# Two transformer blocks on one core: the order of sixteen experts' products, and the rows in which their weights arrive

## The chip, the cores and the metric

The kernel runs on one core of a Trainium2 chip. The metric is the device time of one execution in microseconds (us), as the median of several runs. A profile is one further execution that the hardware profiler took; its engines are PE (TensorE's matmuls), PEld (TensorE's weight loads), DVE (VectorE), ACT (ScalarE), POOL (GpSimd) and SP (SyncE, which here issues transfers only).

## The reference

A sequence of 512 tokens of width 1024 goes through two blocks in float32. The first block (a gated linear recurrence, an mLSTM, a cross attention, an MLP) and the attention half of the second are not touched by the change. What is touched is the second block's expert layer and what follows it:

```python
def expert_choice_ffn(xn, w_router, w_gate, w_up, w_down):   # 16 experts, cap = 64 tokens each
    aff = jax.nn.softmax(jnp.einsum('bsd,de->bse', xn, w_router).astype(jnp.float32), axis=-1)
    top_aff, top_idx = lax.top_k(jnp.swapaxes(aff, 1, 2), cap)
    xg = xn[bidx, top_idx]
    hid = jax.nn.silu(jnp.einsum('becd,edf->becf', xg, w_gate)) * jnp.einsum('becd,edf->becf', xg, w_up)
    y = jnp.einsum('becf,efd->becd', hid, w_down) * top_aff[..., None].astype(xn.dtype)
    return jnp.zeros((B, S, D), dtype=y.dtype).at[bidx, top_idx].add(y)
# then: h = h + sigmoid(rmsnorm(h) @ w_ple_gate) * (p @ w_ple), and a last rmsnorm
```

Each expert has three matrices of 1024 x 1024 in float32, 4 MB each; the sixteen together are 201 MB, and each is read once.

## The kernel before

The residual `x` lies in SBUF as four tiles of 128 tokens. The experts go in pairs, since two times 64 chosen tokens fill 128 partitions. For a pair, `gather` builds a one-hot matrix `oh` on DVE (L1351), and `rows(k)` multiplies it with the tokens on PE, 128 columns of the model at a time (L1360: four matmuls, each of which the profile shows as two); ACT copies each result into `xg` (L1361). `affinities` (L1366) picks the 128 affinities with the same one-hot, and four transposes turn the one-hot into `gT` (L1457).

For each expert, the gate and the up product (L1445) take eight steps `k` each, with 64 tokens as stationary operand and two halves of 512 columns; a step is four matmul records. DVE and ACT make `hd = silu(gate) * up` (L1460 to L1462), PE transposes it (L1465), ACT copies that into `hT` (L1467), and the down product (L1471) takes eight steps more. Its result, times the affinity, is kept in two parts, `yh` (ACT, L1479) and `yl` (DVE, L1480). After the second expert of a pair, `scatter` sends `yh` and `yl` back through `gT` (L1483, L1484), and DVE adds the eight results into `x` (L253). After expert 15 the adding is merged with the first half of the next projection (L1492 to L1510); before that, PE turns `x` into `xT` (L1530). Beside expert 5 the small product `p @ w_ple` is made (`project_p`, L1386).

PSUM has eight banks: four of tag `d` (`pd`: gate, up, scatter), two of tag `s` (`pscore`: down, gather rows, affinities) and two of tag `o` (`pout`: transposes).

Weights arrive in pieces of 1 MB, two steps `k` each, issued on SP's queue (L804, L806). Fifteen buffers in a ring (`wnext` 12, `wlast` 3) take them; six places that are still free at the start (`spare`: `act_hi`, `pp`, four `y4` tiles) take the first extra ones, so that 21 MB can lie ready. In HBM each matrix has rows of 4 KB, so a piece is 256 packets of 4 KB.

The program's text gives priorities. A planner of the framework sets the order of each engine's instructions ahead of the run, from its own estimate of when operands are ready; semaphores then hold each instruction until they are. On the chip each engine follows that order. The order written before is, for each expert: gather (even experts), gate and up, hidden, transposes, down, scatter (odd experts); gather rows are written between the steps of the gate product, and the last pair's gather stands after expert 11's gate and up (L1448).

Of the kernel before, what the change touches and what calls it, by code (L numbers as in the profile page):

```python
# [19 lines left out]
P = 128  # L20
# [15 lines left out]
def two_blocks_kernel(ctx: ExitStack, tc: tile.TileContext, A: dict, out: bass.AP, stage: int = 99):  # L36
# [751 lines left out]
    turn = itertools.cycle(["wnext"] * 12 + ["wlast"] * 3)  # L788
# [7 lines left out]
    def load_pieces(e, got):  # L796

        for n in ("w_exp_gate_2", "w_exp_up_2", "w_exp_down_2"):
            wv = A[n][0, e].rearrange("(k p) f -> p k f", p=P)
            for k in range(0, KT, 2):  # L800
                w = spare.pop(0) if e < 2 and len(got) >= 16 + 4 * e else w8()
                if isinstance(w, list):
                    for i in range(2):
                        nc.sync.dma_start(w[i], wv[:, k + i, :])  # L804
                else:
                    nc.sync.dma_start(w, wv[:, k:k + 2, :])  # L806
                    w = [w[:, 0, :], w[:, 1, :]]
                got += w
                yield

    spare = []
    started = {}

    def start_expert(e, n):

        if e not in started:
            got = []
            started[e] = got, load_pieces(e, got)  # L820
        for _ in itertools.islice(started[e][1], n):
            pass

    def load_expert(e):
        start_expert(e, 12)
        return started[e][0]


    with ExitStack() as blk:
# [440 lines left out]
        open_ring(late, "wnext", 12, side="right")  # L1270
        start_expert(0, 6)

        def more():
            start_expert(0, 8 - 6)
            start_expert(1, 4)
# [32 lines left out]
    with ExitStack() as blk:  # L1308
        pool = blk.enter_context(tc.tile_pool(name="moe", bufs=1, reuse_waits="tile"))
        open_ring(blk, "wlast", 3)  # L1310

        def y4(dt=F32, shape=(D,)):
            return pool.tile([P] + list(shape), dt, name="y4", tag="y4", bufs=5)

        def m2(dt=F32, shape=(T,)):
            return pool.tile([P] + list(shape), dt, name="m2", tag="m2", bufs=4)
# [5 lines left out]
        def pick(ahead=False):  # L1322
            if ahead:
                return m2(shape=(NT, 2, CAP)), y4(shape=(2, KT, CAP))
            return (pool.tile([P, NT, 2, CAP], F32, name="oh", bufs=1),
                    pool.tile([P, 2, KT, CAP], F32, name="xg", bufs=1))

        picked = [pick()]
        w = acts_half(F32, (NT, D), "act_hi")
        spare += [w[:, 0:2, :], w[:, 2:4, :], [y4(), y4()], [y4(), y4()]]  # L1330
# [5 lines left out]
        spare += [w[:, 0:2, :], w[:, 2:4, :]]  # L1336
        ws = load_expert(0)
# [3 lines left out]
        def gather(g):  # L1341

            oh, xg = picked.pop() if picked else pick(ahead=2 * g + 2 == NE)
# [11 lines left out]
            src, sel = (xn[0], oh) if g else (x, scaled)  # L1355

            def rows(k):
# [13 lines left out]
            return oh, xg, rows, affinities  # L1371

        def load_p():
# [4 lines left out]
            return pr, raw  # L1378

        def split8(raw):  # L1380
            hi, lo = w8(dt=F32R), w8(dt=F32R)
            S.copy(hi, raw)
            V.tensor_sub(lo, raw, hi.bitcast(F32))
            return hi, lo

        def project_p(pr, raw):  # L1386
            wh, wl = split8(raw)
            pT = w8((2, 2, T), F32R)
# [41 lines left out]
        oh = xg = None  # L1430
        for e in range(NE):
            if e == NE - 1:
                gfin = row(y4(), A["norm_final_2"])
# [225 lines left out]
```

## Time and profile before

| | us |
|---|---|
| runs: median (lowest, highest) | 1955.38 (1954.65, 1956.43) |
| profiled execution | 1954.67 |
| its span in the profile | 1952.9 |
| PE busy | 1878.2 |
| DVE busy | 919.1 |
| ACT busy | 718.4 |

The span is the time from the first to the last instruction that the profile shows. Busy times overlap between engines. A busy PE is not PE at its peak: matmuls are pipelined and a record holds its drain, so starts must be compared, not lengths. "Idle before" names what released an instruction. The experts begin at 1383.5 us with the first gather, and the last down product ends at 1890 us; 63 us follow.

### The profile page before, as it was taken

What the parts mean: (1) busy time and instruction counts of PE and PEld (TensorE: products, weight loads), DVE (VectorE), ACT (ScalarE), POOL (GpSimd) and SP (SyncE); (2) the same over time, 40 slices, a digit from 0 to 9 for tenths busy, and PEclk for the clock granted to TensorE, in tenths of its full rate; (3) what the DMA queues carried; (4) which work ended last, traced back from release to release, by engine and by line L of the source; (5) the groups of instructions that cost most, each with busy time, mean ns of one, the idle gap of its engine ahead of it and who ended that gap; (6) DMA issues with size and microseconds to landing.
All of it is one profiled execution on the core that took longest, in us unless ns stands there. A gap on an engine that the chain in (4) does not pass through costs nothing. (4 is left out here: it accounts for less than half of the span.)

```text
span 1952.9 us, 24468 instructions
## 1 busy us (share of the span) xinstructions
PE 1878.2 (96%) x9723; PEld 1362.9 (70%) x9723; DVE 919.1 (47%) x1659; ACT 718.4 (37%) x1329; POOL 66.9 (3%) x103
## 2 busy tenths in 40 slices
PE   7999999999999999999999999999699999999998
PEld 6777788888888888887787778887344354444346
DVE  5777777465543443436875564453322111111236
ACT  4454774343332322325665554322121121111134
POOL 0000220000000000002000000000000000000000
PEclk9999999999999999999999999999799999999999
DMA  7222226431233333324222222236889999998951
GB/s 206 55 64 72 56 85 189 131 107 55 73 111 98 97 97 97 97 76 112 73 65 57 74 71 70 86 125 247 325 312 402 375 381 401 406 405 334 409 237 44
DMA packets 178052, 330.88 MB, mean 169 GB/s; under 512 B 10766, under 2 KB 90370, under 8 KB 177938
## 3 DMA queue, kind: packets, MB, share of 16 engines
q1 hardware_dynamic: 177522, 328.91, 48.1%
q8 instruction: 77, 1.26, 0.3%
q0 software_dynamic: 416, 0.41, 0.1%
q14 instruction: 37, 0.30, 0.0%
HBM read 327.19 MB, written 2.10 MB: 169 GB/s over the span
## 5 line engine op out<-in xcount | busy, mean ns | idle before, releaser
L104 DVE TENSOR_TENSOR lo<-raw,hi 128x1024 fp32r<-128x1024 f32 x208 | 253.5, 1221 | 324.5 <-ACT hi L103 321.5
L103 ACT CAST hi<-raw 128x1024 fp32r<-128x1024 f32 x208 | 218.0, 1049 | 417.7 <-PE pd L126 230.7
L124 PE MATMUL pd<-hi,act_hi 128*128 128x512 f32 (+2 forms) x584 | 228.2, 391 | 2.0 <-ACT act_hi L206 1.6
L125 PE MATMUL pd<-lo,act_hi 128*128 128x512 f32 (+2 forms) x584 | 226.5, 388 | 0.8 <-DVE lo L104 0.8
L124 PE MATMUL pd<-act_hi,hi 128*128 128x512 f32 (+1 forms) x592 | 224.2, 380 | 0.5 <-ACT act_hi L206 0.5
L126 PE MATMUL pd<-act_hi,lo 128*128 128x512 f32 (+1 forms) x592 | 224.5, 380 | 0.0
L125 PE MATMUL pd<-act_lo,hi 128*128 128x512 f32 (+1 forms) x592 | 224.3, 379 | 0.0
L1445 PE MATMUL pd<-w,xg 128*64 128x512 f32 x896 | 205.3, 598 | 0.0
L126 PE MATMUL pd<-hi,act_lo 128*128 128x512 f32 (+1 forms) x512 | 199.8, 392 | 0.0
L1445 PEld LDWEIGHTS pd<-w,xg 128*64 128x64 f32 x896 | 60.8, 137 | 109.0 <-issue 100.3
L124 PEld LDWEIGHTS pd<-hi,act_hi 128*128 128x128 f32 x584 | 110.3, 189 | 22.7 <-ACT act_hi L206 3.3
L126 PEld LDWEIGHTS pd<-act_hi,lo 128*128 128x128 f32 x592 | 111.5, 188 | 19.5 <-issue 0.2
L125 PEld LDWEIGHTS pd<-act_lo,hi 128*128 128x128 f32 x592 | 111.5, 188 | 19.4 <-DVE act_lo L207 0.5
L124 PEld LDWEIGHTS pd<-act_hi,hi 128*128 128x128 f32 x592 | 111.1, 188 | 19.9 <-ACT act_hi L206 1.0
L125 PEld LDWEIGHTS pd<-lo,act_hi 128*128 128x128 f32 x584 | 110.2, 189 | 20.1 <-DVE lo L104 1.3
L1471 PE MATMUL pscore<-w,m 128*64 128x512 f32 x464 | 107.9, 607 | 6.7 <-ACT m L1467 6.7
L126 PEld LDWEIGHTS pd<-hi,act_lo 128*128 128x128 f32 x512 | 96.7, 189 | 17.9 <-DVE act_lo L207 0.4
L1480 DVE SCALAR_TENSOR_TENSOR y<-pscore,affs,y 64x512 fp32r<-64x512 f32 x32 | 24.0, 750 | 169.2 <-ACT y L1479 168.9
L253 DVE TENSOR_TENSOR x<-x,pd 128x512 f32<-128x512 f32 x111 | 71.9, 684 | 61.9 <-PE pd L126 56.7
L125 PE MATMUL pd<-lo,hh 128*128 128x512 f32 x256 | 99.7, 390 | 0.0
L124 PE MATMUL pd<-hi,hh 128*128 128x512 f32 x256 | 99.7, 389 | 0.0
L126 PE MATMUL pd<-hi,hl 128*128 128x512 f32 x256 | 99.6, 389 | 0.0
(459 smaller groups left out, 2870.9 us busy)
## 6 DMA issues: line engine op xcount, KB each, us to landing
w<-in_w_exp_gate_dram SPq DMA_DIRECT2D x64, 1024.0 KB, 9.1
w<-in_w_exp_up_dram SPq DMA_DIRECT2D x64, 1024.0 KB, 13.8
w<-in_w_exp_down_dram SPq DMA_DIRECT2D x58, 1024.0 KB, 9.0
raw<-in_w_in_dram SPq DMA_DIRECT2D x80, 512.0 KB, 3.6
raw<-in_w_up_dram SPq DMA_DIRECT2D x32, 512.0 KB, 4.2
raw<-in_w_down_dram SPq DMA_DIRECT2D x32, 512.0 KB, 3.6
raw<-in_w_xkv_dram SPq DMA_DIRECT2D x16, 512.0 KB, 4.9
raw<-in_w_out_dram SPq DMA_DIRECT2D x16, 512.0 KB, 3.7
```

Source lines behind the costliest of these rows:

```text
L103: S.copy(hi[:, :size], raw[:, :size])
L104: V.tensor_sub(lo[:, :size], raw[:, :size], hi[:, :size].bitcast(F32))
L124: PE.matmul(ps, ah, bh, start=first, stop=False)
L125: PE.matmul(ps, ah, bl, start=False, stop=False)
L126: PE.matmul(ps, al, bh, start=False, stop=last)
L253: return lambda t, ps: V.tensor_add(x[:, t, c:c + 512], x[:, t, c:c + 512], ps)
L1445: PE.matmul(ps[64 * half:64 * half + 64, :], xg[:, e % 2, k, :], ws[i + k][:, 512 * half:512 * half + 512], start=(k == 0), stop=(k == KT ...
L1471: PE.matmul(py[64 * half:64 * half + 64, :], hT[:, k % 4, 64 * (k // 4):64 * (k // 4) + 64], ws[16 + k][:, 512 * half:512 * half + 512], s ...
L1480: V.scalar_tensor_tensor(yl[r0:r0 + 64, 512 * half:512 * half + 512], src, sc, h.bitcast(F32), op0=OP.mult, op1=OP.subtract)
```

## The change

The experts are pipelined by one: `hidden(e)` (gate and up of expert e) stands ahead of `down(e-1)`, and `turned(e)` (the transposes and their copy) behind it. Scatters of the pair before are called between every second step of an odd expert's gate and up product. Rows of the next gather are called between the steps of the down product of the pair's first expert (for the last pair, the turns of `x`). Gather rows go to `pout`, four in one bank, and no longer to `pscore`; the turned one-hot goes to `pscore`. Loads come in the order of use, gate and up of e+1 ahead of down of e, and a counter (`room`) issues each when its buffer's user is written. The host stacks the three matrices into one tensor in which a piece is contiguous, 8 KB for each partition. `y4` has 4 buffers for 5, `m2` 3 for 4, and `gT` a tile of its own. The three work buffers of the `p` product are now taken when its loads are issued.

```diff
+    order = [(0, m) for m in range(2)]
+    for e in range(1, NE):
+        order += [(e, 0), (e, 1), (e - 1, 2)]
+    order.append((NE - 1, 2))
+    order = [(e, m, q) for e, m in order for q in range(KT // 2)]
+    pieces = {(e, m): [] for e in range(NE) for m in range(3)}
+    homes = {}
+    loads = iter(enumerate(order))
+    room = [WNEXT + WLAST]
+
+    def load(n):
+        for i, (e, m, q) in itertools.islice(loads, n):
+            wv = A["w_exp"][e, m, q]
+            if i in homes:
+                w = homes[i]
+            else:
+                w = w8()
+                room[0] -= 1
...
+                nc.sync.dma_start(w.rearrange("p a b -> p (a b)"), wv.rearrange("p a b -> p (a b)"))
...
+    def used(e, m):
+        room[0] += sum(r for _, r in pieces.pop((e, m))) // 2
+        load(max(0, room[0]))
...
             def rows(k):
-                ps = pscore()[:, :P]
+                j = k % 4
+                if j == 0:
+                    ps[0] = pout()
                 for t in range(NT):
-                    PE.matmul(ps, src[:, t, k * P:(k + 1) * P], sel[:, t, :], start=(t == 0), stop=(t == NT - 1))
-                S.activation(xg[:, :, k, :], ps.rearrange("p (e s) -> p e s", e=2), AF.Copy, scale=gcol[:, k:k + 1])
+                    PE.matmul(ps[0][:, j * P:(j + 1) * P], src[:, t, k * P:(k + 1) * P], sel[:, t, :],
+                              start=(t == 0), stop=(t == NT - 1))
+                S.activation(xg[:, :, k, :], ps[0][:, j * P:(j + 1) * P].rearrange("p (e s) -> p e s", e=2), AF.Copy,
+                             scale=gcol[:, k:k + 1])
...
+            def back():
+                gT = pool.tile([P, T], F32R, name="gT", bufs=1)
+                pt = pscore()
+                for t in range(NT):
+                    PE.transpose(pt[:, t * P:(t + 1) * P], oh[:, t, :], ident)
+                S.copy(gT, pt)
+                return gT
...
+        def hidden(e, xg, between):
             pg, pu = pd(), pd()
-            for i, ps in ((0, pg), (8, pu)):
+            for m, ps in enumerate((pg, pu)):
                 for k in range(KT):
...
+                    for f in between.get(KT * m + k, ()):
+                        f()
+            for m in range(2):
+                used(e, m)
             hd = m2()
             S.activation(hd, pg, AF.Sigmoid)
             V.tensor_mul(hd, hd, pg)
             V.tensor_mul(hd, hd, pu)
+            return hd
+        def turned(e, hd):
             pt = pout()
             for i in range(4):
                 PE.transpose(pt[:, i * P:(i + 1) * P], hd[:, i * P:(i + 1) * P], ident)
-            hT = m2(shape=(4, P))
-            S.copy(hT, pt.rearrange("p (a b) -> p a b", a=4))
+            hT[e] = m2(shape=(4, P))
+            S.copy(hT[e], pt.rearrange("p (a b) -> p a b", a=4))
+        def down(e, yh, yl, between):
+            h = hT.pop(e)
             py = pscore()
             for k in range(KT):
...
+                for f in between.get(k, ()):
+                    f()
+            used(e, 2)
...
+        hd = hidden(0, xg, each([lambda k=k: rows(k) for k in range(1, KT)], range(KT - 1)))
+        turned(0, hd)
+        for e in range(1, NE):
             if e == 5:
+                room[0] -= 5
+            todo = [lambda t=t, n=n: scatter(t, n, pd()) for n in range(2) for t in range(NT)] if e % 2 and e > 1 else []
+            hd = hidden(e, xg, each(todo, range(0, 16, 2)))
...
+            more = {}
+            if e % 2:
+                affinities()
+                gT = back()
+                yh, yl = y4(F32R), y4(F32R)
+                if e + 1 < NE:
+                    xg, rows, affinities, back = gather((e + 1) // 2)
+                    more = each([lambda k=k, f=rows: f(k) for k in range(KT)], range(KT))
+                else:
+                    wgr = [load_gate(k) for k in range(0, KT, 2)]
+                    xT = [w8((4, T)) for _ in range(2)]
+                    more = each([lambda t=t, i=i: turn_x(t, i) for t in range(NT) for i in range(2)], range(KT))
+            if e == 6:
+                pp = project_p(*praw)
+                room[0] += 5
+            down(e - 1, yh, yl, more)
+            if e == 5:
+                praw = load_p()
+            turned(e, hd)
+        gfin = row(y4(), A["norm_final_2"])
+        down(NE - 1, yh, yl, {})
...
+    w = np.stack([given.pop(f"w_exp_{n}_2")[0] for n in ("gate", "up", "down")], 1)
+    given["w_exp"] = w.reshape(NE, 3, KT // 2, 2, P, D).transpose(0, 1, 2, 4, 3, 5)
```

## Rows read from the trace of the kernel before

**Rows 1.** The page: busy tenths of PE and DMA in 40 slices.
```profile
PE   7999999999999999999999999999699999999998
...
DMA  7222226431233333324222222236889999998951
```

**Rows 2.** Window: length, busy us of PE, PEld, DVE, ACT, POOL; clock, DMA, GB/s.
```profile
1387.00:1890.00 503.00, 480.06 (x2394) 216.78 (x2392) 89.35 (x151) 88.71 (x191) 0.00 (x0) 0.99 0.95 374
```

**Rows 3.** L1445's waits (us, times), then waits of SP (total, times, longest).
```profile
  DMA w<-in_w_exp_gate_dram: 2.3, 8
...
SPq L806 <- PE pd L1445: 258.3, 111, 19.7
```

**Rows 4.** Waits of PE, 1387 to 1890: total us, times, longest.
```profile
PE pout L1465 <- DVE m L1462: 11.5, 12, 2.8
PE pscore L1471 <- ACT m L1467: 6.7, 14, 0.9
PE pscore L1360 <- ACT xg L1361: 1.6, 4, 0.5
PE pscore L1360 <- ACT y L1361: 1.1, 1, 1.1
```

**Rows 5.** PE's timeline, experts 8 and 9: start, length, line, operation, idle before.
```profile
1661.70 5.37 PE L1445 MATMUL pd<-w,xg 128*64 128x512 f32 x24
1667.87 0.66 PE L1465 MATMUL pout<-ident,m 128*128 128x128 f32 x4 [0.79 <-DVE m L1462]
1669.25 7.09 PE L1471 MATMUL pscore<-w,m 128*64 128x512 f32 x32 [0.73 <-ACT m L1467]
1676.17 13.90 PE L1445 MATMUL pd<-w,xg 128*64 128x512 f32 x64
...
1692.19 1.94 PE L1471 MATMUL pscore<-w,m 128*64 128x512 f32 x8 [0.24 <-ACT m L1467]
1694.06 1.16 PE L1360 MATMUL pscore<-oh,act_hi 128*128 128x128 f32 x8
1695.15 1.94 PE L1471 MATMUL pscore<-w,m 128*64 128x512 f32 x8
...
1703.87 0.94 PE L1360 MATMUL pscore<-oh,act_hi 128*128 128x128 f32 x6
```

**Rows 6.** PE's timeline, end of expert 6.
```profile
1600.98 0.64 PE L1457 MATMUL pout<-ident,oh 128*128 128x128 f32 x4
...
1614.97 13.90 PE L1445 MATMUL pd<-w,xg 128*64 128x512 f32 x64
```

**Rows 7.** PE's timeline: affinities of expert 2, scatters after experts 7 and 13.
```profile
1460.13 8.80 PE L1445 MATMUL pd<-w,xg 128*64 128x512 f32 x40
...
1469.86 1.07 PE L1445 MATMUL pd<-w,xg 128*64 128x512 f32 x2
...
1643.53 1.20 PE L1483 MATMUL pd<-y,m 128*128 128x512 f32 x4
...
1645.48 0.38 PE L1360 MATMUL pscore<-oh,act_hi 128*128 128x128 f32 x2
...
1649.49 4.51 PE L1445 MATMUL pd<-w,xg 128*64 128x512 f32 x20
...
1834.41 1.21 PE L1483 MATMUL pd<-y,m 128*128 128x512 f32 x4 [0.78 <-ACT y L1479]
...
1839.99 1.51 PE L1445 MATMUL pd<-w,y 128*64 128x512 f32 x6
```

**Rows 8.** PE's timeline, end of expert 15.
```profile
1877.61 1.09 PE L1530 MATMUL pout<-ident,x 128*128 128x128 f32 x8
...
1882.93 7.09 PE L1471 MATMUL pscore<-w,m 128*64 128x512 f32 x32 [0.68 <-ACT m L1467]
```

**Rows 9.** DMA: a burst of 2 KB rows, a stretch of 4 KB rows.
```profile
DMA packets 285, 0.55 MB, mean 367 GB/s; under 512 B 16, under 2 KB 16, under 8 KB 285
...
DMA packets 2120, 8.20 MB, mean 410 GB/s; under 512 B 120, under 2 KB 120, under 8 KB 2119
```

More of the change, by code (lines that the diff above doesn't have):

```diff
@@ L1370, in affinities @@
                         S.copy(affs[64 * half:64 * half + 64, e:e + 1], ps[64 * j:64 * j + 64, e:e + 1])
-            return oh, xg, rows, affinities
+            def back():
[5 more added lines that the diff above has]
+                return gT
+            return xg, rows, affinities, back
         def load_p():
@@ L1481, in two_blocks_kernel @@
                                        op0=OP.mult, op1=OP.subtract)
-            def scatter(t, n, ps):
-                PE.matmul(ps, gT[:, t * P:(t + 1) * P], yh[:, 512 * n:512 * n + 512], start=True, stop=False)
-                PE.matmul(ps, gT[:, t * P:(t + 1) * P], yl[:, 512 * n:512 * n + 512], start=False, stop=True)
-                add_to_x(512 * n)(t, ps)
-            last = e == NE - 1 and stage > 7
-            if e % 2 and not last:
-                for n in range(2):
-                    for t in range(NT):
-                        scatter(t, n, pd())
@@ L1511, in two_blocks_kernel, with scatter, each @@
-            if e == 4:
-                praw = load_p()
+        def scatter(t, n, ps):
+            PE.matmul(ps, gT[:, t * P:(t + 1) * P], yh[:, 512 * n:512 * n + 512], start=True, stop=False)
+            PE.matmul(ps, gT[:, t * P:(t + 1) * P], yl[:, 512 * n:512 * n + 512], start=False, stop=True)
+            add_to_x(512 * n)(t, ps)
+        def each(fs, places):
+            b = {}
+            for f, i in zip(fs, places):
+                b.setdefault(i, []).append(f)
+            return b
@@ L1513, in two_blocks_kernel, with turn_x @@
+        def turn_x(t, i):
+            ps = pout().rearrange("p (a b) -> p a b", a=4)
+            for k in range(4):
+                PE.transpose(ps[:, k, :], x[:, t, (4 * i + k) * P:(4 * i + k + 1) * P], ident)
+            S.copy(xT[i][:, :, t * P:(t + 1) * P], ps)
+        xg, rows, affinities, back = gather(0)
+        rows(0)
+        hd = hidden(0, xg, each([lambda k=k: rows(k) for k in range(1, KT)], range(KT - 1)))
+        turned(0, hd)
+        for e in range(1, NE):
             if e == 5:
-                pp = project_p(*praw)
@@ new lines, in two_blocks_kernel @@
+            if e == 6:
[7 more added lines that the diff above has]
+        down(NE - 1, yh, yl, {})
+        zh, zl = [[w8((4, T), F32R) for _ in range(2)] for _ in range(2)]
+        wg = []
+        pss = [pd() for _ in range(NT)]
+        todo = [(t, n) for n in range(2) for t in range(NT)]
+        for k in range(KT):
+            ps = pout()
+            PE.matmul(ps, yh[:, k * P:(k + 1) * P], gT, start=True, stop=False)
+            PE.matmul(ps, yl[:, k * P:(k + 1) * P], gT, start=False, stop=True)
+            zk, hi = xT[k // 4][:, k % 4, :], zh[k // 4][:, k % 4, :]
+            V.tensor_add(zk, zk, ps)
+            S.copy(hi, zk)
+            V.tensor_sub(zl[k // 4][:, k % 4, :], zk, hi.bitcast(F32))
+            if k % 2:
+                wg.append(split_gate(k // 2, wgr[k // 2]))
+                gate_step(pss, k // 2)
+                for _ in range(2):
+                    scatter(*todo.pop(0), pscore())
```

139 lines of the change are left out of this document (34 added, 105 removed).

## The prediction

> **What bounds the kernel now.** I read the page's slices first, then the windows, then the waits, then PE's timeline. The slices say that PE and the DMA engines are both full in the last third of the span [rows 1], so one must find which of them waits for the other. The window over the experts, 1387 to 1890 us, has PE busy 480.06 of 503 us at 374 GB/s [rows 2]. The waits decide. PE's gate and up products stood for a landing 8 times, 2.3 us in all, while the loads stood 258.3 us, 111 times, for those same products to free a buffer [rows 3]. Weights lie ready and transfers wait for PE: the stage is paced by TensorE and by what stops it. Two waits stop it: the transposes of the hidden tile wait 11.5 us for VectorE's product, and the down product 6.7 us for ScalarE's copy of the transposes [rows 4]. That is one chain per expert: gate and up, VectorE, four transposes, copy, down.
>
> How much time lies behind the chain? 374 GB/s over 503 us are 188.1 MB; in a full stretch the queue moves 410 GB/s [rows 9], so these bytes need 459 us and could end at 1846. PE can save 44 us before transfers set the end, even if rows move no faster than now.
>
> **The change, part by part.** Sums are for the profiled execution, 1954.67 us with a span of 1952.9; the median of the runs is 1955.38, so 0.7 is added at the end. Steps between starts: an expert matmul 0.213 us (13.90 for 64 less 5.37 for 24, over 40), a gather matmul or a transpose 0.11 (1.16 for 8 less 0.94 for 6, over 2) [rows 5], a scatter matmul 0.244 (1643.53 to 1645.48 for 8) [rows 7].
>
> *The hidden chain goes.* In the new order gate and up of expert e+1 run before the down product of e, and the transposes of e+1 after it, so the chain lies beside a product of some 7 us. Its price today, from start to start: expert 8 goes from 1661.70 to 1669.25, 7.55 us for 24 matmuls and four transposes worth 5.55: 2.00 lost. Expert 9 goes from 1676.17 to 1692.19, 16.02 for 64 matmuls and eight transposes worth 14.51: 1.51 [rows 5]. There are 5 like the first (experts 4, 8, 10, 12, 14) and 7 like the second (1 to 13, odd). Expert 6 is worse: 1600.98 to 1614.97 is 13.99 for eight transposes and 32 matmuls worth 7.70, 6.29 lost [rows 6]; the longest single wait, 2.8, is there [rows 4]. Expert 15: 1877.61 to 1882.93 is 5.32 for 28 transposes worth 3.08, 2.24 lost [rows 8]. Experts 0 and 2 have other work there already. Sum 10.0 + 10.6 + 6.3 + 2.2 = 29.1. The four transposes still interrupt products, and such a visit costs 0.33 (affinities inside the gate product: 1460.13 to 1469.86 is 9.73 for 40 and 8 matmuls worth 9.40 [rows 7]), so 14 x 0.33 = 4.6 stays. Gain 24.5.
>
> *The scatter moves into the next gate and up product.* Expert 13's scatter waited for its results and VectorE's adds: 1834.41 to 1839.99 is 5.58 for 16 matmuls worth 3.90 [rows 7]. Gain 1.7. The other six lose little today, as gather matmuls fill them: 1643.53 to 1649.49 is 5.96 for 16 scatter and 16 gather matmuls worth 5.66 [rows 7], 0.30 each, 1.8 in all. Woven in, 56 scatters of two matmuls each interrupt a product. As single visits at the gather's 0.38 (below) that is 21.3 - 1.8 = +19.5; with two to a visit (two of four pd banks are free beside gate and up) 28 x 0.33 - 1.8 = +7.4; if they fell only where PE stands, -1.8. I take +7.4, nearest to today's rows, which have scatters in clusters.
>
> *The gather moves into the down product.* It is interleaved already: 8 down matmuls and a row of 8 gather matmuls take 2.96 (1692.19 to 1695.15), worth 2.58, so 0.38 a visit [rows 5]. I count 49 visits to products in the timeline; the new program writes 63 (7 in the first gate product, 56 in down products): +5.3 as written, 0 if the planner joins rows as it does today, -12 if it joined most. I take half, +2.6. The waits of today's rows for ScalarE, 1.6 + 1.1 [rows 4], go, as 0.85 of product stands between two rows: gain 2.7.
>
> *Small ones.* The 8 turns of x become visits: 8 x 0.33 = +2.6. The last expert's transposes stand right ahead of its down product with nothing beside them: 1.38 (1667.87 to 1669.25) less 0.44 of transposes [rows 5], +0.9. The down product needs one of two score banks, and the affinities and the turned one-hot take both just ahead of it: 0 to 0.4 eight times, I take 1.0. One y4 and one m2 buffer fewer: in the tail at most three gated tiles live, and y4 holds the last pair, the final gain and junk; 0, at worst one 0.7 us VectorE step. The five p buffers leave ten pieces of the ring, as now, loads come in the order of use, and SP only loads here: 0, covered by weights that lie ready.
>
> *8 KB packets.* No weight row of 8 KB is in the trace. Full stretches give 367 GB/s at 2 KB and 410 at 4 KB [rows 9]: 89 and 160 ns a packet, which goes on to about 301 ns at 8 KB, an estimate of 436 GB/s. From below stands the 2 KB row, 367. I take the nearest, 410, and 0 us: PE waits for no weights, and the 44 us are cover. Without it the stage would take 188.1 MB at the rate that comes.
>
> Sum: removed 24.5 + 1.7 + 2.7 = 28.9; added 7.4 + 2.6 + 2.6 + 0.9 + 1.0 = 14.5. Net -14.4: 1940.3, and 1941 against the median. With the high ends (19.5, 5.3, 2.6, 0.9, 3.2) it is +2.6; with the low ends (-1.8, 0, 2.6, 0.9, 0) -27.2, and -39 if the gather's visits are joined as well.
>
> A page bears on the visits. A visit costs 0.33 and 0.38 us in the trace [rows 5, 7]. The Trainium skill, "TensorE: Matmul & The Clock Gate", Part 2, has PE's queue draw the next weight load ahead of running matmuls, so that it overlaps. By that rule visits would be free, as in the fast rival; the trace disagrees on the price.
>
> **The rivals.**
> 1. *Gather rows queue on one bank (slower).* Four rows now share one pout bank, and each is copied out alone. Before, a row with no product ahead of it waited up to 0.5 for ScalarE's copy [rows 4]. 48 rows follow another in the same bank; all of them back to back cost 48 x 0.5 = 24: 1965. It decides from 29 of the 48. For it: the planner puts ready work where it expects PE to stand. Against: the program has a product step between two rows. The Trainium skill, "PSUM — Partial Sum Buffer", "PSUM bank collisions raise a hardware error", wants PE's writes and another engine's reads kept apart by bank, not by address. By that rule disjoint columns would wait too; no row here shows two engines in one bank. Chance 0.12.
> 2. *Work is regrouped (faster).* The planner sets PE's order; today gather rows stand among scatters that were written earlier [rows 7]. With more ready work it may join rows and scatters: the low ends, 27 to 39 less, 1917 to 1929. Against it: a single xg, and two free pd banks. Chance 0.17.
> 3. *The chain stays in part.* If the planner sets the transposes right behind their own product, half of the 24.5 remains: -2.2, 1953. For it: they become ready early. Against: the down product is written first and its weights are there. Chance 0.15.
> 4. *Transfers set the pace (slower).* If 8 KB rows moved at the 2 KB row's 367, 188.1 MB would take 512.5 us, 9.5 more than the stage now: 1965. It decides below 385 GB/s (188.1 MB in 488.6 us). Against it: the rate rises with the size. Chance 0.06.
>
> **The numbers.** Forecast 0.50, 1941, its own range 1932 to 1950. About 0.2% (3.9 us) is what a measurement tells from no change. Faster (under 1951.5): forecast 0.49, rival 2 0.17, rival 3 0.07, rival 1 in part 0.01, 0.74. Within: 0.01, rival 3 0.07, rivals 1 and 4 0.02 each, 0.12. Slower: rival 1 0.09, rival 4 0.04, rival 3 0.01, 0.14. The range 1924 to 1959 leaves out the fast end of rival 2 and the full price of rivals 1 and 4, some 0.2 together.
>
> **What would show it.** Right: PE's waits for VectorE and ScalarE ahead of transposes and down products, 18.2 us now, fall under 4; the stage's 503 us become some 489; the loads still wait for PE; the 63 us after the last down product stay. Rival 1 shows as gather matmuls that wait for xg's copies, rival 3 as the old two waits at half their sum, rival 4 as weight loads that wait for landings. The forecast is wrong if a visit to a product costs much other than 0.33 to 0.38, or if PE's order is not the program's.

## The result, and the profile after

The changed kernel takes 1970.21 us (median of four runs, 1969.27 to 1972.07) against 1955.02 for the kernel before on the same chip: a ratio of 1.0080, 95% interval [1.0068, 1.0093]. It is slower by some 15 us, where 14 less were forecast. Times of experiments are given as ratios to the kernel before, run on the same chip, which took 1953.5 to 1955.9 us there; differences in us are differences of these ratios times 1955. The interval of one ratio is some 0.0013 to either side, so the difference of two is known to some 3.6 us (an estimate from these intervals).

First the window over the experts, from the first gate product to the end of the last down product (columns as in [rows 2]), and the tail behind it:

```profile
1387.00:1906.00 519.00, 499.53 (x2394) 212.56 (x2392) 92.37 (x151) 88.82 (x191) 0.00 (x0) 0.99 0.89 359
...
1906.00:1969.00 63.00, 53.40 (x250) 42.64 (x248) 44.35 (x77) 31.72 (x62) 4.50 (x8) 0.98 0.09 34
```

The stage grew from 503 to 519 us with the same 2394 matmuls, the tail is the 63 us that it was. PE is busy 96% of the stage, so "busy" doesn't show the loss: it lies inside the records. The waits in the stage (engine, line, releaser; us in all, times, longest) answer to [rows 3, 4]:

```profile
PE pout L1465 <- DVE m L1459: 3.9, 5, 0.8
PE pscore L1381 <- ACT affs L1374: 3.8, 5, 0.8
PE pout L1504 <- ACT w L1505: 3.1, 2, 2.9
PE pd L124 <- ACT w L206: 2.7, 1, 2.7
PE pout L1362 <- ACT xg L1364: 2.1, 4, 0.5
PE pd L125 <- DVE w L1395: 1.4, 1, 1.4
PE pd L1491 <- DVE y L1486: 1.1, 4, 0.3
PE pscore L1475 <- ACT m L1467: 0.7, 1, 0.7
...
SPq L822 <- PE pd L1450: 230.2, 113, 15.8
SPq L822 <- PE pscore L1475: 161.9, 51, 11.4
```

The old two waits fell from 18.2 us to 4.6 (L1465, L1475). Others came or grew: the turned one-hot behind the affinities (L1381, none before), the turns of x (L1504, 0.4 before) and p's product (L124 and L125, 0.3 before). A scatter's 1.1 (L1491) is no more than the scatters waited before (1.4). No landing is among them, and the loads still wait for PE.

Waits explain little, so the time was counted from start to start: in each run of equal matmuls, from its first start to the first start of the next run, less the number of matmuls times their dense step (0.214 us an expert matmul, 0.112 a gather matmul or a transpose, 0.219 a scatter). What is left over is "lost", and belongs to the work that cuts into the expert products: it is put down to the work that starts next, or, where expert matmuls start next, to the work that ends. "Rows" include the 64 matmuls ahead of the first product. Worked out from all PE records of the stage of each kernel:

```
lost us, stage         rows  scatter  hidden    affin.+   p's      turns  other  sum   cuts into
                                      transp.   one-hot   product  of x                products
before                 26.1    2.7     23.6      4.6       2.1      0.9    2.2   62.2     74
after                  25.3   21.9     10.3      8.1       8.7      3.5    0.5   78.3    123
unpiped                22.0   18.2     20.1      2.2       8.8      0.8    0.4   72.7    126
as_written             27.4   21.2      5.2      5.1       5.4      2.2    0.4   66.8    144
cuts_few                7.0   -0.5      6.0      2.4       9.6      1.5    0.8   26.8     38
cuts_spread            12.2   11.0      5.2      2.4       8.2      1.5    0.8   41.2     80
cuts_few_unpiped        8.8   -0.9     29.1      3.3       8.5      1.5    0.8   51.2     38
```

From before to after the sum rises by 16.1, and the end of the last down product moves from 1890.0 to 1906.0. The hidden chain gave 13.3 back; the scatter took 19.2, p's product 6.6, affinities and one-hot 3.5, the turns 2.6. Where scatters and rows share a cut, as they did before, the split between them depends on the rule of counting; together they rose by 18.4 (28.8 to 47.2). PE's timeline (start, length, line, count, idle before) shows a woven scatter in expert 7:

```profile
1613.78 0.50 PE L1490 MATMUL pd<-y,gT 128*128 128x512 f32 x1
1614.12 0.40 PE L1491 MATMUL pd<-y,gT 128*128 128x512 f32 x1
1614.44 1.94 PE L1450 MATMUL pd<-w,xg 128*64 128x512 f32 x8
1616.31 0.50 PE L1490 MATMUL pd<-y,gT 128*128 128x512 f32 x1
```

From 1613.78 to 1616.31 are 2.53 us for eight expert matmuls (1.71) and two scatter matmuls (0.44): 0.38 lost without any recorded wait, and 49 such cuts are in the stage, where before had one: its scatters stood in blocks with gather rows [rows 7].

### The profile page after: what moved, and what is told of

It reads as the page before. It is cut to its first block, busy times and chain, and to the rows that moved or that the text cites. A ratio compares the mean times of both kernels' runs of the same rounds, so it can differ in the third digit from the quotient of the medians.

```text
span 1969.0 us, 24454 instructions
## 1 busy us (share of the span) xinstructions
PE 1897.0 (96%) x9723; PEld 1357.7 (69%) x9723; DVE 921.9 (47%) x1659; ACT 718.3 (36%) x1329; POOL 66.8 (3%) x103
## 4 chain that ended last, share of the span: by engine, by line
PE 82%; DVE 8%; ACT 5%; issue 2%; DMA 2%; POOL 1%; SPq 0%; POOLq 0%; ACTq 0%; DVEq 0%
PE pd L125 16%; PE pd L126 16%; PE pd L124 16%; PE pd L1450 12%; PE pscore L1475 6%; PE pout L1362 4%; DVE lo L104 1%; ACT hi L103 1%; PE pd L1490 1%; PE pout L1126 1%; PE pd L1491 1%; PE pout L204 1%; POOL rs L188 1%; PE pscore L400 1%; PE pout L1023 1%
## 5 line engine op out<-in xcount | busy, mean ns | idle before, releaser
L1450 PE MATMUL pd<-w,xg 128*64 128x512 f32 x984 | 230.2, 601 | 0.0
L124 PE MATMUL pd<-hi,act_hi 128*128 128x512 f32 (+2 forms) x584 | 227.8, 390 | 1.5 <-ACT act_hi L206 1.1
L125 PE MATMUL pd<-lo,act_hi 128*128 128x512 f32 (+2 forms) x584 | 226.6, 389 | 0.7 <-DVE lo L104 0.7
L124 PE MATMUL pd<-act_hi,hi 128*128 128x512 f32 (+1 forms) x592 | 224.2, 380 | 0.5 <-ACT act_hi L206 0.5
L125 PE MATMUL pd<-act_lo,hi 128*128 128x512 f32 (+1 forms) x592 | 224.2, 379 | 0.0
L1450 PEld LDWEIGHTS pd<-w,xg 128*64 128x64 f32 x984 | 65.7, 137 | 122.0 <-issue 117.9
L124 PEld LDWEIGHTS pd<-hi,act_hi 128*128 128x128 f32 x584 | 110.2, 189 | 22.1 <-ACT act_hi L206 2.8
L126 PEld LDWEIGHTS pd<-act_hi,lo 128*128 128x128 f32 x592 | 111.5, 188 | 19.5 <-issue 0.2
L125 PEld LDWEIGHTS pd<-act_lo,hi 128*128 128x128 f32 x592 | 111.6, 188 | 19.3 <-DVE act_lo L207 0.6
L124 PEld LDWEIGHTS pd<-act_hi,hi 128*128 128x128 f32 x592 | 111.1, 188 | 19.9 <-ACT act_hi L206 1.0
L125 PEld LDWEIGHTS pd<-lo,act_hi 128*128 128x128 f32 x584 | 110.3, 189 | 20.1 <-DVE lo L104 1.2
L1475 PE MATMUL pscore<-w,m 128*64 128x512 f32 x504 | 121.7, 603 | 1.2 <-ACT m L1467 0.7
L126 PEld LDWEIGHTS pd<-hi,act_lo 128*128 128x128 f32 x512 | 96.6, 189 | 18.2 <-DVE act_lo L207 0.6
L125 PE MATMUL pd<-lo,hh 128*128 128x512 f32 x256 | 99.7, 390 | 0.0
L124 PE MATMUL pd<-hi,hh 128*128 128x512 f32 x256 | 99.7, 389 | 0.0
```

Source lines behind the costliest of these rows:

```text
L124: PE.matmul(ps, ah, bh, start=first, stop=False)
L125: PE.matmul(ps, ah, bl, start=False, stop=False)
L126: PE.matmul(ps, al, bh, start=False, stop=last)
L1450: PE.matmul(ps[64 * half:64 * half + 64, :], xg[:, e % 2, k, :], w[:, 512 * half:512 * half + 512], start=(k == 0), stop=(k == KT - 1))
L1475: PE.matmul(py[64 * half:64 * half + 64, :], h[:, k % 4, 64 * (k // 4):64 * (k // 4) + 64], w[:, 512 * half:512 * half + 512], start=(k == ...
```

## The experiments

A "cut" is a place where another kind of matmul stands inside or between expert products; the planner makes TensorE's order, so the cuts are those of the order it made.

**1. Scatters two to a place.**

```diff
-            hd = hidden(e, xg, each(todo, range(0, 16, 2)))
+            hd = hidden(e, xg, each(todo, [4 * (i // 2) for i in range(8)]))
```

> The changed kernel with the eight scatters of a pair of experts written two to a place (four places in the gate and up product) instead of eight places. Theory of visits: each time another kind of matmul cuts into an expert product costs some 0.35 us, and in the changed kernel's trace the scatters lose 21.9 us over their dense price (21.9 of 78 lost in the stage) against about 6.5 before. Here TensorE's order has 111 cuts into products instead of 123, so 12 x 0.35 = 4.2 us less, and up to 2 more where two scatters now share a cut: 1964 to 1966 against 1970 for the changed kernel and 1955 for the one before. Rival, that it is the count of the scatters and not of the cuts that costs (VectorE's adds, banks): no change, 1969 to 1971.

Measured 1.0046 [1.0032, 1.0060], 6.6 us under the changed kernel (0.0034 of 1955). The scatter's loss fell from 21.9 to 16.1 in its trace; rows and p's product lost some 1 us less each, all else stayed. The count of cuts matters, and not the count of scatters. (The 6.5 "before" in the expectation counts the scatters' loss by another rule than the table's 2.7.)

**2. Rows in two banks. 3. Rows at one place.**

```diff
-                j = k % 4
-                if j == 0:
-                    ps[0] = pout()
+                j = 0
+                ps[0] = pout()
...
-                    more = each([lambda k=k, f=rows: f(k) for k in range(KT)], range(KT))
+                    more = each([lambda k=k, f=rows: f(k) for k in range(KT)], [1] * 8)
```

The first part is run 2, both are run 3.

> The changed kernel with each gather row in a pout tile of its own (two banks in turn) instead of four rows in one bank; the places stay. Theory of visits: the number of cuts stays (125 against 123), so 1969 to 1971. Rival, the shared bank: the weight load ahead of a gather row stood 21.2 us for ScalarE's copy of the row before in the changed kernel's trace, the matmul itself 2.1; if that is what a cut costs, the time falls by 2 at the least and by up to 21: 1949 to 1968.

> The same two banks in turn, and all eight gather rows of a pair written at one place of the down product. Theory of visits: 99 cuts instead of 125, 26 x 0.35 = 9 us less than with two banks and eight places, less at most 2 us of waits for ScalarE's copies inside the block: 1960 to 1963. The rival of the shared bank sees no difference from two banks alone. A third, that ScalarE's copies set the pace of a block (0.36 us each against 0.9 of matmuls), would make it slower than two banks alone.

Two banks: 1.0073 [1.0061, 1.0086], 1.4 us less and inside the interval. One place: 1.0030 [1.0019, 1.0042], 8.4 us below two banks. The shared bank, which was the first rival of the prediction, is not the cause; cuts are.

**4. p ahead.** p is loaded at expert 4; `split_p` (the split and the transposes of `project_p`) stands ahead of `hidden(6)`.

```diff
-            if e == 5:
+            if e == 4:
                 room[0] -= 5
+            if e == 6:
+                split_p(*praw)
...
-            if e == 5:
+            if e == 4:
                 praw = load_p()
```

> The changed kernel with p loaded one expert earlier, and its split and transposes written ahead of the gate and up product of expert 6, so that a product of 14 us lies between them and p's matmuls. In the changed kernel's trace the p product lost 8.7 us (2.7 for ScalarE's copy of p's transposes, 1.4 for VectorE's low part, and what follows at a lower clock) against 0.9 before. Theory that this is a cost of its own, from the place of the p product: 7 to 8 us less, 1962 to 1964. Rival, that the gap only stands for the loads that stopped there (the five p buffers; 230 GB/s around 1610) and would be paid elsewhere: 1969 to 1971.

Measured 1.0058 [1.0045, 1.0071], 4.3 us less: half of what was expected. p's own loss fell from 8.7 to 2.3, but the planner, with p gone from there, set one more group of transposes right behind its product (hidden transposes 10.3 to 12.3).

**5. Packets of 4 KB.**

```diff
-            wv = A["w_exp"][e, m, q]
+            wv = A["w_exp_%s_2" % ("gate", "up", "down")[m]][0, e].rearrange("(k p) f -> p k f", p=P)[:, 2 * q:2 * q + 2, :]
```

> The changed kernel with the experts' weights in the layout of before (packets of 4 KB); nothing else changes, TensorE's order is the same. Theory that PE sets the pace: the changed kernel's stage of 522 us needs 188.1 MB, 360 GB/s, well under the 410 of full 4 KB stretches, so no change: 0 to 1 us slower than the changed kernel (about 1.008 of before, 1969 where before is 1953.5). Rival, that the 8 KB packets carried part of the time after the p product, where the trace shows 418 to 422 GB/s for 120 us on end: 2 to 5 us slower, with waits for landings of 5 us or more.

Measured 1.0076 [1.0064, 1.0089]: no difference. The changed kernel doesn't live on its transfers.

**6. Turns early.** xT lies in `act_hi`; scatters and turns stand in expert 15's gate and up.

```diff
...
+            else:
+                w = acts_half(F32, (2, 4, T), "act_hi")
+                xT = [w[:, i] for i in range(2)]
+                todo += [lambda t=t, i=i: turn_x(t, i) for i in range(2) for t in range(NT)]
+                hd = hidden(e, xg, each(todo, range(16)))
```

> The changed kernel with the end of the stage rearranged: xT in the storage of the normalised x that is free by then, expert 13's scatters one to each of the first eight steps of expert 15's gate and up, and the eight turns of x behind them in the same product, instead of ahead of the last two down products. In the changed kernel's trace 3.1 us go ahead of the turns (ScalarE's copy of a turn stands behind the copies of the down product's result), 1.9 between the turns and the last transposes, 1.1 behind these. Theory that this is a cost of its own: 4 to 5 us less, a ratio to before of 1.0055 to 1.006. Rival: the scatters and turns, crowded, wait for VectorE's adds (0.69 each) and cut as often, so nothing is won: 1.008.

Measured 1.0054 [1.0041, 1.0067], 5.1 us less, as the first theory said (4 to 5).

**7. The pipelining alone undone.**

```diff
-    for e in range(1, NE):
-        order += [(e, 0), (e, 1), (e - 1, 2)]
+    order = [(e, m) for e in range(NE) for m in range(3)]
...
+            turned(e, hd)
...
+            down(e, yh, yl, more)
```

> The pipelining alone undone: each expert's transposes and down product come right behind its own gate and up, the loads in that order; scatters woven into gate and up, gather rows into the down products, 8 KB packets and the p buffers stay. TensorE's order has 127 cuts into products against 123. (The first weights get two homes fewer, which only the first loads feel.) What it gives is the worth of the pipelining by itself. Theory: the hidden chain's waits come back, some 14 to 21 us, less what the planner fills: 12 to 20 us slower than the changed kernel, a ratio of 1.014 to 1.018. Rival, that the planner fills the chain with woven work as it did before (rows ahead of a down product, the next expert's gate): within 5 us of the changed kernel, 1.006 to 1.010.

Measured 1.0043 [1.0031, 1.0056]: 7.2 us faster than the changed kernel, outside both theories. The chain's waits did come back, 9.5 and 3.9 us in this trace's waits of PE:

```profile
PE pout L1461 <- DVE m L1455: 9.5, 12, 0.8
PE pd L124 <- ACT w L206: 4.7, 1, 4.7
PE pscore L1471 <- ACT m L1463: 3.9, 6, 0.9
```

They cost 9.8 (20.1 against 10.3), but affinities and one-hot cost 5.9 less, scatter and rows 7.0, turns 2.7. In the changed order the down product in progress holds one score bank, so the one-hot's transposes must take the bank of the affinities and wait for their copies (3.8 us above); here both score banks are free at that place. Run 10 below, with the affinities in a `pd` bank, has no such wait. Why rows and scatters cost 7.0 less with as many cuts is not shown.

**8. Transposes pinned.**

```diff
-                PE.transpose(pt[:, i * P:(i + 1) * P], hd[:, i * P:(i + 1) * P], ident)
+                tc.keep_in_program_order(
+                    PE.transpose(pt[:, i * P:(i + 1) * P], hd[:, i * P:(i + 1) * P], ident))
```

> The changed kernel with the four transposes of the hidden tile pinned behind the down product that is written ahead of them. In the changed kernel the planner set them right behind their own gate and up product five times, each with 1.02 us lost to VectorE's product (5.1 in all). TensorE's order now has 117 cuts against 123. Theory of a chain that stayed in part: 5 us for the waits and 2 for six cuts, 7 less, a ratio of 1.0043 to 1.005. Rival, that the wait moves to the next thing in the way (ScalarE's copy of the transposes ahead of the next down product, or a row's copy): 0 to 2 less, 1.007 to 1.008.

Measured 1.0047 [1.0033, 1.0060], 6.5 us less, as expected. Five times the planner had put the transposes straight behind their own gate and up, as here for expert 4 in the changed kernel, with the one-hot's wait behind it:

```profile
1506.29 13.95 PE L1450 MATMUL pd<-w,xg 128*64 128x512 f32 x64
1521.04 0.66 PE L1465 MATMUL pout<-ident,m 128*128 128x128 f32 x4 [0.79 <-DVE m L1459]
1521.63 1.94 PE L1475 MATMUL pscore<-w,m 128*64 128x512 f32 x8
1523.49 1.06 PE L1370 MATMUL pscore<-aff,oh 128*128 128x16 f32 x8
1525.32 0.66 PE L1381 MATMUL pscore<-ident,oh 128*128 128x128 f32 x4 [0.77 <-ACT affs L1374]
```

**9. Everything pinned as written.** Every matmul and transpose of the stage goes through `pin`.

```diff
+    def pin(i):
+        return tc.keep_in_program_order(i) if written else i
```

> The changed kernel with TensorE's instructions of the stage pinned to the order in which the program writes them, nothing else changed. It tells whether the loss is the planner's reordering or the order of the program. There are 144 cuts into products instead of 123, 21 x 0.35 = 7 us more; the five waits of the transposes for VectorE go (5 us less); p's product stands right behind its transposes, 3 to 6 us more. Theory of cuts: 1.009 to 1.013 of before. Rival, that the planner spoilt an order that would have brought the forecast gain: 0.993 to 1.000.

Measured 1.0024 [1.0015, 1.0033], 11 us faster than the changed kernel and 4.7 slower than before: neither theory. There are 21 cuts more, as expected, yet rows and scatter lose only 1.4 more in sum, since a written scatter costs 0.38 (21.2 over 56) and the planner's 0.45 (21.9 over 49); the transposes' waits (5.1) and a good third of p's and of the one-hot's losses are gone. The planner's order cost 11 us; the program's own order is still slower than before.

**10. Few cuts, planner's order. 11. Few cuts, pinned. 12. The block in the middle.** Runs 3, 4 and 6 together, affinities in a `pd` bank, the scatters at the rows' place (the turned one-hot in two buffers). In 11 the order is pinned, affinities and one-hot stand in one cut inside gate and up, and the first rows stand ahead of the first product. Run 12 is run 11 with the block behind four of the down product's eight steps, where run 11 has it behind two.

```diff
-            todo = [lambda t=t, n=n: scatter(t, n, pd()) for n in range(2) for t in range(NT)] if e % 2 and e > 1 else []
+            todo = [lambda t=t, n=n, y=(gT, yh, yl): scatter(t, n, pd(), y) for n in range(2) for t in range(NT)] if e % 2 and e > 1 else []
...
+            if e % 2:
+                between[8] = [affinities, lambda f=back: got.append(f())]
...
-                    more = each([lambda k=k, f=rows: f(k) for k in range(KT)], range(KT))
+                    more = each([f for p in itertools.zip_longest([lambda k=k, f=rows: f(k) for k in range(KT)], todo) for f in p if f], [1] * 16)
```

> The changed kernel with what the runs so far point to, the order left to the planner: gather rows in two banks and all written at one place of the down product, the scatters of the pair before written at the same place (the turned one-hot in two buffers), p one expert earlier with its split ahead, affinities in a pd bank, the end of the stage as in the run with the turns early. 70 cuts instead of 123: 53 x 0.35 = 18.5 us less; p 4, turns 5, the affinities' wait 4 to 5 less: some 32 less in all, a ratio of 0.990 to 0.993 to before. Rival, that transfers set the pace as soon as PE saves more than 10 us: 0.997 to 1.002, with waits for landings.

> The same parts, with TensorE's order of the stage pinned: a gate and up product of an odd expert is cut once (affinities and turned one-hot), the down product beside it once (eight rows and eight scatters in turn), the products of the even experts not at all, the transposes between products; the first eight rows ahead of the first product. 38 cuts instead of 123: 85 x 0.35 = 30 us less; the transposes' waits 5, p 4 to 6, turns 5, affinities 5 less: 49 to 51 in all, a ratio of 0.981 to 0.984. Rival, that transfers become the bound: 188.1 MB at 420 GB/s are 448 us, and the stretches where the loads stop (the first 67 us at 267 GB/s, the p buffers) add some 40: a stage of 488 instead of 522, 0.988 to 0.992, with PE's waits for landings up from 3 us to 15 or more.

> As the run before, the block of rows and scatters in the middle of the down product (behind eight of 16 matmuls of the program) instead of behind four. Theory: the same number of cuts, the same time within 2 us. Rival, that the block's first scatters wait for VectorE (the hidden product's three steps of 2.4 us still hold their banks when the block comes after four): 3 to 7 us less than the run before (seven such blocks, up to 1 us each).

Measured 0.9868 [0.9854, 0.9881], 0.9817 [0.9804, 0.9830] and 0.9821 [0.9807, 0.9834]. Run 11 (1918.61 us) is 51 us under the changed kernel and 36 under the one before, as the sum of the parts said; the place of the block doesn't matter. Run 10, with 69 cuts, came out 6 us better than its theory (0.990 to 0.993), and outside both; why is not shown. A block of run 11's trace:

```profile
...
1718.35 1.16 PE L1366 MATMUL pout<-oh,act_hi 128*128 128x128 f32 x8
1719.27 0.48 PE L1497 MATMUL pd<-y,gT 128*128 128x512 f32 x1
1719.58 0.40 PE L1498 MATMUL pd<-y,gT 128*128 128x512 f32 x1
1719.81 1.05 PE L1366 MATMUL pout<-oh,act_hi 128*128 128x128 f32 x8
...
1721.17 1.05 PE L1366 MATMUL pout<-oh,act_hi 128*128 128x128 f32 x8
```

A row and a scatter take 1.36 us in the block (1719.81 to 1721.17), against 1.33 dense: rows and scatters alternate at no price.

After these runs it was open what a cut costs alone, what the pipelining is worth alone, whether the packets matter where PE is faster, and what p's transposes cost; runs 13 to 16 change one thing each in run 11.

**13. The block spread.**

```diff
-... [1] * 16)
+... [i * KT // (KT + len(todo)) for i in range(KT + len(todo))])
```

> The run with few cuts (1918.6, 0.9817 of before) with the rows and scatters of each block spread again, one row and one scatter to each of the eight steps of the down product, order pinned, nothing else changed: 80 cuts against 38. It is the price of a cut by itself. Theory: 42 x 0.35 = 14.7 us more, a ratio of 0.988 to 0.990. Rival, that the few-cuts run won by the waits that went and not by the cuts: 0 to 4 us more, 0.982 to 0.984.

Measured 0.9890 [0.9875, 0.9905], 14.3 us more than run 11 for 42 cuts: 0.34 each (0.25 to 0.43 by the two intervals). The table's sums differ by 14.4, of which 1.0 lies in the rows ahead of the first product, so the traces give 0.32. None of PE's recorded waits grew by more than 0.2 us. The same row and scatter now, between steps of the down product:

```profile
1730.09 1.08 PE L1481 MATMUL pscore<-w,m 128*64 128x512 f32 x4
1731.10 1.16 PE L1366 MATMUL pout<-oh,act_hi 128*128 128x128 f32 x8
1732.01 0.47 PE L1497 MATMUL pd<-y,gT 128*128 128x512 f32 x1
1732.33 0.40 PE L1498 MATMUL pd<-y,gT 128*128 128x512 f32 x1
1732.65 1.08 PE L1481 MATMUL pscore<-w,m 128*64 128x512 f32 x4
```

2.56 us from 1730.09 to 1732.65, less four expert matmuls (0.86), leave 1.70 for what took 1.36 in the block. PEld's timeline over the same stretch:

```profile
1731.10 0.97 PEld L1366 LDWEIGHTS pout<-oh,act_hi 128*128 128x128 f32 x8 [0.81 <-issue]
...
1732.10 0.19 PEld L1498 LDWEIGHTS pd<-y,gT 128*128 128x128 f32 x1
1732.65 0.20 PEld L1481 LDWEIGHTS pscore<-w,m 128*64 128x64 f32 x4 [0.36 <-issue]
```

Inside the cut, the weight load of the second scatter matmul starts 0.23 us ahead of its matmul (1732.10 and 1732.33). At both edges of the cut the load starts together with its matmul (1731.10, 1732.65), after PEld had done nothing for 0.81 and 0.36 us and had waited for no semaphore.

**14. Run 11 without the pipelining.** The same `order` as in run 7, the same 38 cuts.

> The run with few cuts with the pipelining alone undone: transposes and down product of an expert right behind its own gate and up, loads in that order, the same 38 cuts (two homes fewer for the first weights). It is the worth of the pipelining where nothing else covers the chain. Theory of the prediction's step: 14 experts, some 1.0 for VectorE's product and 0.93 for ScalarE's copy each, 24 to 27 us more, a ratio of 0.994 to 0.996. Rival, as in the run that undid the pipelining of the changed kernel, that it is worth little (below 12 us): 0.982 to 0.988.

Measured 0.9952 [0.9939, 0.9964], 26.4 us more than run 11, in the range of the first theory. The transposes account for 23.1 of it in the table; in the traces the first product also starts 4.5 us later (1395.8 against 1391.3), which has no part in the chain. Its waits:

```profile
PE pout L1467 <- DVE m L1461: 12.0, 15, 0.9
PE pscore L1477 <- ACT m L1469: 10.9, 16, 0.7
```

**15. Run 11 with 4 KB.** The edit of run 5.

> The run with few cuts in the layout of before, packets of 4 KB. Its stage needs 188.1 MB in some 470 us, 400 GB/s, close to the 410 that full stretches of 4 KB give; with 8 KB they give 418 to 422. Theory that weights now set part of the pace: 3 to 10 us slower, 0.983 to 0.987, with PE's waits for landings above 10 us. Rival, that the ring of 15 pieces still covers it: 0 to 1 us, 0.981 to 0.983.

Measured 0.9859 [0.9845, 0.9872], 8.2 us more than run 11. PE's waits for landings are 4.2 us, fewer than the 10 expected, and none in run 11; its weight loads wait 12.0 for landings (4.2, 4.1 and 3.7) where run 11's wait 6.0. A window of this run, then one of run 11, then run 11's longest waits of SP:

```profile
1650.00:1700.00 50.00, 50.00 (x268) 23.76 (x266) 10.66 (x18) 7.17 (x18) 0.00 (x0) 1.00 1.03 409
```

```profile
1650.00:1700.00 50.00, 50.00 (x268) 23.73 (x266) 10.65 (x18) 7.17 (x18) 0.00 (x0) 1.00 1.01 420
```

```profile
SPq L827 <- DMA w<-in_w_exp_dram: 159.1, 80, 3.5
SPq L827 <- PE pd L1456: 118.7, 68, 17.6
SPq L827 <- PE pscore L1481: 80.2, 28, 12.4
```

In run 11 the loads still wait for PE (118.7 + 80.2 us, 392 in the changed kernel), but they also wait 159.1 for earlier loads, where the changed kernel shows 2.6 at most: transfers run at 420 GB/s and set part of the pace, so the 2.7% that the larger packets add are worth 8 us there and nothing in the changed kernel.

**16. Run 11 with p's transposes in the product.**

```diff
+            if e == 6:
+                between = {3: [lambda: split_p(*praw, (0, 1))], 7: [lambda: split_p(*praw, (2, 3))]}
```

> The run with few cuts with p's transposes inside expert 6's gate and up product, two and two, instead of ahead of it, where its trace shows 6.8 us lost behind them (they wait 5.3 for VectorE's work on p). Theory: these 6.8 go, two cuts of 0.35 come: 6 us less, a ratio of 0.978 to 0.979. Rival, that the loads which the p buffers hold up are late next, so PE waits for landings in their stead: 0 to 2 us less, 0.9805 to 0.982.

Measured 0.9848 [0.9834, 0.9861], 6.1 us slower than run 11, against both theories. The wait itself stayed and came later: only PE's order is pinned, and ACT and DVE have p's split behind the sigmoid and the first product step of the same gate there (DVE's part starts at 1558.8, in run 11 at 1551.7). The p buffers came free later, the loads stopped, and PE's waits now hold landings, of which run 11 had none:

```profile
PE pout L209 <- DVE w L212: 5.4, 1, 5.4
PE pd L1457 <- DMA w<-in_w_exp_dram: 2.1, 4, 0.6
PE pscore L1482 <- DMA w<-in_w_exp_dram: 1.2, 2, 0.7
```

## Why the prediction was wrong

**The step that failed** is "The scatter moves into the next gate and up product", with "28 x 0.33 - 1.8 = +7.4" taken and "single visits ... +19.5" kept as the upper end. The trace shows 49 cuts and +19.2 (2.7 to 21.9). The price of a visit was right: 0.32 to 0.34 by run 13, 0.38 for a written scatter by run 9. The number of visits was not: the program writes 56 single scatters, and the prediction counted 28 pairs because today's rows have scatters in clusters. With the 1.7 for expert 13 its forecast for the scatter was +5.7. Of the 14 more gather visits it took half, and the trace has 57 cuts with rows against 50, so that step held. Counted as written, the stage goes from 74 cuts to 144; the planner made 123.

**The hidden chain**, "Gain 24.5", came as 13.3. Run 14 shows that the chain is worth 23 to 26 us where nothing else covers it, so its mechanism stands. In the kernel before it lost 23.6, not 29.1: the prediction counted whole stretches, which also hold one-hot transposes, turns of x and, at expert 6, a lower clock. PE's wait of 2.8 us there ends at 1604.42, and in the next 5 us the granted clock was 0.50 (1.2 of 2.4 GHz; third column from the end of the window). The down product behind it took 8.87 us, where expert 8's took 7.09 [rows 5]:

```profile
1604.00:1609.00 5.00, 3.85 (x12) 1.60 (x14) 0.37 (x1) 0.59 (x1) 0.00 (x0) 0.50 1.03 411
```

The 16 visits of the transposes themselves cost 5.2 in run 9, against 4.6 forecast, and the planner left five waits of 1.0 standing, which is rival 3 in part: pinning them gave 6.5 (run 8). 23.6 less 5.2 and 5.1 are the 13.3.

**The p buffers**, "0, covered by weights that lie ready", cost 6.6. The cover was there for the loads; the price arose on PE. p's split and transposes now stand right ahead of p's product, and ACT and DVE have the copies of the down product's result in front of them, with nothing for PE beside it. PE's timeline in the changed kernel:

```profile
1596.64 1.34 PE L124 MATMUL pd<-w,w 128*128 128x512 f32 x4 [2.72 <-ACT w L206]
1599.36 0.80 PE L125 MATMUL pd<-w,w 128*128 128x512 f32 x1 [1.38 <-DVE w L1395]
...
1601.66 0.63 PE L125 MATMUL pd<-w,w 128*128 128x512 f32 x1
1602.08 0.63 PE L126 MATMUL pd<-w,w 128*128 128x512 f32 x1
...
1604.98 0.39 PE L124 MATMUL pd<-w,w 128*128 128x512 f32 x1
1605.21 0.39 PE L125 MATMUL pd<-w,w 128*128 128x512 f32 x1
```

The matmuls at 1602 start 0.42 apart, those at 1605 0.23: the clock, below, took some 2 us of the 8.7 (an estimate from these starts).

**Smaller terms.** Score banks: 1.0 forecast, 3.5 measured (affinities and one-hot), by the wait that run 7 lacks. Turns of x: +2.6 forecast and +2.6 measured, but by another cause: of the 3.5 that they lost, 2.9 is one wait for ACT's copy, which stands behind the copies of the down product's result (run 6 took 5.1 off, with the last transposes). Gather: -0.1 forecast, -0.8 measured. The tail and the packets: 0 and 0, right; 8 KB rows moved at 420 GB/s, between the 410 and the 436 of the prediction. All terms together make up the 30.5 us between the forecast -14.4 and the +16.1 of the traces: scatter 13.5, chain 10.3 (with its 0.9 for the last transposes), p 6.6, score banks 2.5, less 2.4 for the gather and the rest.

**Rivals.** The shared bank is refuted by run 2. The Trainium skill, "PSUM — Partial Sum Buffer", in "PSUM bank collisions raise a hardware error", wants PE's writes and another engine's reads apart by bank. No run here shows a price of that. PEld's idle time ahead of rows is put down to ACT's copies in the changed kernel and, all but the same, in run 2, where each row has a bank of its own:

```profile
PEld pout L1362 <- ACT xg L1364: 21.2, 26, 1.4
PEld pout L1361 <- ACT xg L1363: 20.2, 22, 1.4
```

It is mostly the 0.81 us that PEld stands at the edge of a cut in any case: in 18 of the 26 it is this long, and the copy had ended some 0.5 us before. The matmuls waited 2.1 us for copies in both runs. Regrouping (rival 2) did not occur: the planner made cuts, and made them irregular. Transfers (rival 4) set no pace here, and do in run 11.

The Trainium skill, "TensorE: Matmul & The Clock Gate", Part 2, has the next weight load drawn ahead of running matmuls, under two conditions that it names. By that rule a cut would be free, as the prediction says; the trace of run 13 agrees inside a cut (0.23 us ahead) and disagrees at its edges (0.00).

**Why the range was missed as well.** All high ends together gave +2.6 us. Waits that the planner's order makes (five transposes, the one-hot, p, in all about 11 us by run 9) had no upper bound in the sum, although the prediction itself named "if PE's order is not the program's" as what would make it wrong.

What stays open is why the load doesn't come ahead at the edge of a cut. What is lost there can be counted. Expert matmuls start two at a time, a pair every 0.43 us, so 0.214 is a mean of their starts. At the cuts of run 13 that open with a row and close with a scatter, the last pair starts 0.53 us ahead of the row (0.10 lost), the first two row matmuls stand 0.21 apart instead of 0.11 (0.10), the product goes on 0.33 behind the last scatter matmul instead of 0.22 (0.11), and its second pair follows the first by 0.48 (0.05): 0.36 in all (medians over all such edges). The weights of expert matmuls are 64 columns wide and those of all other work 128; no run changes this width alone, so whether it is the reason is not shown.

## What to carry to other kernels

Count how often a product is cut, as the program writes it, before asking what a wait is worth: here a cut costs 0.34 us with no wait in the trace, so 85 cuts fewer are worth 29 us by that price (an estimate), about as much as the whole pipelining. Work that fills gaps should be woven in as blocks, and where a planner sets the order, read its order for each wait that is to go and pin it. A part that is worth nothing while another bound holds (8 KB packets: 0 us) can be worth 8 us after that bound has moved, so try it again there.

## What the runs showed of the hardware

- A cut into an expert product costs 0.34 us (14.3 us for 42 cuts); rows and scatters in turn inside a block cost 0.02 to 0.03 a pair (1.36 against 1.33). At the edges of a cut the weight load starts with its matmul, inside a cut up to 0.23 ahead of it (run 13).
- Loads in rows of 8 KB run at 420 GB/s where the same loads in 4 KB run at 409 (windows of runs 11 and 15), with DMA engines full in both.
- After PE had stood 2.7 us at p's product (until 1596.64), the granted clock fell; from 1599 to 1604 it was 0.50, 1.2 of 2.4 GHz, with PE busy 4.64 of these 5 us. Windows of the changed kernel, clock in the third column from the end:

```profile
1594.00:1599.00 5.00, 1.34 (x4) 0.67 (x4) 3.49 (x3) 2.01 (x4) 0.00 (x0) 0.85 0.14 57
1599.00:1604.00 5.00, 4.64 (x13) 3.71 (x14) 1.91 (x5) 1.33 (x3) 0.00 (x0) 0.50 0.71 233
1604.00:1612.00 8.00, 8.00 (x35) 6.58 (x35) 0.00 (x0) 3.52 (x6) 0.00 (x0) 0.98 0.31 119
```
